# Two decoder layers on one core: a written opening, the block diagonal of the keys by ScalarE, and the first inverses' lower blocks between pieces of the second group's values

## The chip, the cores and the metric

The kernel runs on one core of a Trainium2 chip. The metric is the device time of one execution in microseconds; the time of a kernel is the median of several runs. A core has TensorE (PE, matmuls; PEld is its weight load), VectorE (DVE), ScalarE (ACT), GpSimd (POOL) and SyncE (SP), which issues all DMAs of this kernel. Each engine works through its own queue in order.

## The reference

A trunk of two layers works on x, 256 tokens by 2048 columns, in float32. Cut to what matters:

```python
h = _rmsnorm(x, gains[0])
# layer 0: combined projection 2048 -> 4096: q | k | v (8 differential heads) and u (S5 input)
proj = h @ w_in
m = concatenate([_diff_attention(q, k, v, ...), _s5(u, ...)]) @ w_out
# layer 1: RWKV-7 time mixing, 32 heads of 64
w_log = -softplus(-(w0 + tanh(xw @ w1) @ w2)) - 0.5
decay = exp(-exp(w_log))
a = sigmoid(a0 + (xa @ a1) @ a2)
kk = heads(k * k_k); kk = kk / max(norm(kk), 1e-12)
k = k * (1 + (a - 1) * k_a)
state = state * w_t + sa * b_t + v_t * k_t        # sa = state @ (-kk_t), b_t = kk_t * a_t
# every layer
x = x + _rmsnorm(m, gains[1])
x = x + _rmsnorm(_swiglu(_rmsnorm(x, gains[2]), ...), gains[3])
```

## The kernel before

**Weights.** All weight matrices are packed on the host into chunks of eight 128x128 blocks in the order of use. `chunk_load` (L358) loads one chunk of 512 KB into `wr` (SP), rounds it to a high half `wh` on ScalarE (L367), and takes the low half `wl = wr - wh` on VectorE (L368), or on POOL for the gate weights. Each of the three tags has three buffers. Activations are split into halves by `split` (L440): ScalarE writes the high one (L446), VectorE the low one (L450 or L452). Every product is then three matmuls: high x high, high x low, low x high.

**Order.** The instructions are written in program order with priorities (`high_priority`), and a list scheduler puts them into the queues of the engines; it also hands out the buffers of each tag. `strict = True` keeps TensorE's instructions in the order in which they are written. `fill(n)` in the values stage issues pieces of other work until n units are spent; a piece (one block row for one half of the tokens, three matmuls of 512 columns) is worth 2. Priorities of `mid()` and `hi()` put work ahead of what is written before it.

**The opening** (`even`, L818). x comes transposed, in five loads with the first three chunks between them (`LX`). For each of 16 row blocks, `split` makes the two halves with the gain, and `Acc.add` (L531) squares the block on ScalarE (L534) and adds the squares on POOL (L536). `rms_bc` (L459) sums them with eight matmuls, takes the power on POOL and spreads the result R over the partitions. `k_outer` (L432) multiplies the first four column blocks of u, 16 steps of 12 matmuls, into four PSUM banks. TensorE's order is not strict here. `s5_setup` (L948) computes the S5 coefficients from the constants `ce` by a chain of small VectorE operations, and `s5_tables` (L980) builds tables on POOL. Behind the opening, `main()` runs v, q, k and u tiles on TensorE while two side programs, attention and S5, are woken by counts of TensorE work (`SEQ`, `L0`, `LI`, `LS`).

**RWKV keys** (`rwkv_keys`, L1395). For each of 16 pairs of heads, `gates` (L1549) computes decays and factors into the tile `E` (tag H), and `pair` (L1592) multiplies the key projection into it. `pair` then builds a block diagonal `bd` of E (L1629, POOL; one buffer, since `NB = 1`), which TensorE multiplies with E to give the matrix `ak`, stored to DRAM (L1635). After pair 8 (`I0`), `inverse` (L1637) of the first half of the heads inverts the two diagonal 32x32 blocks of each ak by a chain of VectorE operations (L1661, L1662) in two buffers of the tag XI. `inverse2` (L1672) makes the lower block from them: twelve loads (L1681 to L1683) into two buffers of XI, 64 small matmuls, a copy, 64 more, a copy (L1699), and four stores (L1702). `I1 = 16` puts it behind the 16 pairs. Then come the values of the first group and `inverse` of the second half of the heads.

**RWKV values** (`rwkv_values`, L1729; TensorE strict). `chunk_in` (L1828) loads the inputs of one chunk of 64 tokens (T, CH, QB, MV), multiplies QB with CH and masks the result on VectorE; `chunk` (L1876) does the state's step. `FILL` lists the work that is put between: the other groups' values and the output projection. `chunk_in` of the first chunk is followed by `fill(FI)`, with `FI = 20`, then by the 16 chunk steps; the lower blocks of the second half come in step 6 (`S2`).

## Time and profile before

| what | value |
|---|---|
| median of 3 runs | 2608.89 us (2600.57 to 2609.81) |
| the profiled execution, its own time | 2606.43 us |
| its span, first to last instruction | 2604.6 us |
| mean granted TensorE clock | 0.975 |

All durations below come from the profiled execution. The page gives busy time by engine, a strip of 40 slices, the DMA queues, the chain of work that ended last, and the costliest groups of instructions by line. The other views used are the table of stretches (busy time of each engine between two moments, with the granted clock and what the DMA moved), the timeline (instructions in order of time; in brackets, how long the engine stood idle before it and what released it), the groups of one stretch by line, and the list of waits. "pg<-Z,wh" names the tile that an instruction writes and those that it reads; SPq is SyncE's queue of DMA issues. Matmuls overlap, so the distance of two starts says more than the duration of one. The engines idle most at these moments: the first 43 us, 76 to 320 us, and 1440 to 1565 us.

### The profile page before, as it was taken

The numbers are of one execution on the slowest core, as the hardware profiler recorded it, in microseconds if no ns is written. First come the engines' busy times: TensorE is split into PE (matmuls) and PEld (weight loads), VectorE is DVE, ScalarE is ACT, GpSimd is POOL, SyncE is SP. The second block draws the span as 40 slices with busy tenths as digits, with TensorE's granted clock in tenths as the row PEclk, the third lists the DMA queues.
The fourth block names the chain that finished last, engine by engine and source line by source line (L and its number), as shares of the span: only waits on it lengthen the run. The fifth ranks groups of instructions, "written<-read, shape, count | busy, mean of one in ns | idle before, by whom it ended". The sixth has DMA issues, their size and how long they took to land. (4 is left out here: it accounts for less than half of the span.)

```text
span 2604.6 us, 37350 instructions
## 1 busy us (share of the span) xinstructions
PE 2476.1 (95%) x14155; PEld 2081.8 (80%) x14155; DVE 1632.4 (63%) x2369; ACT 1205.3 (46%) x1808; POOL 408.3 (16%) x664
## 2 busy tenths in 40 slices
PE   7898799999999999998899889999999999999998
PEld 7786688788888888887799778887788888888886
DVE  7888985555555554445569978777555555555444
ACT  5343264644444444444666543443554444444433
POOL 4776621000000000000215630111100000000000
PEclk9898899999999999999999989999999999999999
DMA  6333256655555556664468677765555555555564
GB/s 218 114 114 103 80 178 199 203 187 186 192 187 186 192 186 200 200 224 161 154 216 248 206 224 197 207 200 171 202 187 186 189 190 186 186 190 190 194 206 162
DMA packets 221892, 481.93 MB, mean 185 GB/s; under 512 B 78736, under 2 KB 110736, under 8 KB 219920
## 3 DMA queue, kind: packets, MB, share of 16 engines
q1 hardware_dynamic: 221712, 479.55, 57.5%
q8 instruction: 111, 1.82, 0.3%
q14 instruction: 69, 0.57, 0.1%
HBM read 451.69 MB, written 27.79 MB: 184 GB/s over the span
## 5 line engine op out<-in xcount | busy, mean ns | idle before, releaser
L368 DVE TENSOR_TENSOR wl<-wr,wh 128x1024 fp32r<-128x1024 f32 x760 | 939.8, 1238 | 790.9 <-ACT wh L367 787.6
L367 ACT CAST wh<-wr 128x1024 fp32r<-128x1024 f32 x768 | 806.3, 1051 | 1023.7 <-PE pb L305 729.3
L305 PE MATMUL pg<-wh,Z 128*128 128x512 f32 x1664 | 641.2, 397 | 2.8 <-DVE Z L450 2.4
L305 PE MATMUL pb<-wh,Z 128*128 128x512 f32 x1408 | 554.0, 394 | 4.1 <-DVE Z L450 4.1
L305 PEld LDWEIGHTS pg<-wh,Z 128*128 128x128 f32 x1664 | 313.8, 189 | 72.8 <-issue 3.4
L305 PE MATMUL pg<-wl,Z 128*128 128x512 f32 x832 | 324.9, 391 | 0.4 <-DVE wl L368 0.4
L305 PEld LDWEIGHTS pb<-wh,Z 128*128 128x128 f32 x1408 | 264.9, 188 | 62.4 <-DVE Z L450 5.0
L305 PE MATMUL pb<-wl,Z 128*128 128x512 f32 x704 | 273.7, 389 | 0.0
L305 PE MATMUL pg<-wh,PP 128*128 128x512 f32 x576 | 225.6, 393 | 0.0
L305 PE MATMUL pb<-wh,PP 128*128 128x512 f32 x576 | 225.4, 393 | 0.0
L305 PEld LDWEIGHTS pg<-wl,Z 128*128 128x128 f32 x832 | 157.1, 189 | 34.5 <-DVE wl L368 1.2
L305 PE MATMUL pg<-wh,MX 128*128 128x512 f32 x504 | 174.9, 410 | 2.6 <-DVE X L1816 1.9
L305 PE MATMUL pg<-MX,wh 128*128 128x256 f32 x896 | 168.5, 286 | 6.7 <-ACT wh L367 4.0
L305 PE MATMUL pg<-Z,wh 128*128 128x256 f32 x736 | 146.3, 301 | 15.1 <-ACT wh L367 11.9
L305 PEld LDWEIGHTS pb<-wl,Z 128*128 128x128 f32 x704 | 132.5, 188 | 29.6
L305 PEld LDWEIGHTS pg<-MX,wh 128*128 128x128 f32 x896 | 139.9, 192 | 8.4 <-ACT wh L367 4.7
L305 PEld LDWEIGHTS pg<-Z,wh 128*128 128x128 f32 x736 | 120.5, 204 | 27.1 <-issue 14.8
L305 PE MATMUL pg<-MX,wl 128*128 128x256 f32 x448 | 128.1, 288 | 5.0 <-DVE wl L368 4.9
L305 PEld LDWEIGHTS pb<-wh,PP 128*128 128x128 f32 x576 | 108.2, 188 | 23.4
L305 PEld LDWEIGHTS pg<-wh,PP 128*128 128x128 f32 x576 | 108.2, 188 | 23.4
L500 POOL TENSOR_TENSOR ts<-ts,mhalf 128x1 f32<-128x1 f32 x6 | 3.3, 553 | 759.0 <-DVE ts L499 759.0
L305 PEld LDWEIGHTS pg<-wh,MX 128*128 128x128 f32 x504 | 96.7, 192 | 24.6 <-DVE X L1816 2.8
(429 smaller groups left out, 3639.1 us busy)
## 6 DMA issues: line engine op xcount, KB each, us to landing
wr<-wst SPq DMA_DIRECT2D x776, 512.0 KB, 3.4
dr<-H SPq DMA_DIRECT2D x16, 512.0 KB, 4.2
CH<-dr SPq DMA_DIRECT2D x16, 512.0 KB, 5.2
dr<-X SPq DMA_DIRECT2D x6, 1024.0 KB, 4.8
X<-dr SPq DMA_DIRECT2D x6, 1024.0 KB, 5.6
dr<-ak SPq DMA_DIRECT2D x16, 256.0 KB, 4.1
ln<-lnb SPq DMA_DIRECT2D x8, 512.0 KB, 4.7
S<-s5bc SPq DMA_DIRECT2D x4, 512.0 KB, 6.7
```

The lines of the kernel that those rows point to most:

```text
L305: self.pe(self.nc.tensor.matmul(out, lhsT, rhs, start=start, stop=stop))
L367: self.gated(nc.scalar.copy(h, r))
L368: self.gated((nc.gpsimd if pool else nc.vector).tensor_tensor(l, r, h.bitcast(F32), op=ALU.subtract))
L500: self.nc.gpsimd.tensor_tensor(r, ms, self.mhalf[:, 0:1], op=ALU.pow)
```

## The change

Four things are changed.

1. **The opening is written out.** TensorE's order is strict from the start. 54 (`W0`) matmuls on a tile of zeros come first. The split of row block k + 4 is written behind step k. The sum of squares is taken from x in row form: two loads of 1 MB (`cx`), two squares of 128x2048 on ScalarE with their sum, and the mean and power as columns; the 16 squares, 14 additions and 8 sum matmuls go. `behind` holds a DMA or an activation until a given chunk's load or cast has been issued on the same engine: the row loads behind chunks 3 and 4, `ce` behind 5, the first two S5 tables behind 6 and 7, the squares behind the casts of 4 and 5. `LX` now puts chunks 1 and 2 one place earlier among the blocks of x.
2. **The block diagonal** is copied by ScalarE (`BE = "a"`).
3. **The gates.** The scaling of the decay's exponent (L1568) leaves VectorE: ScalarE adds 1 and the factor goes into the scale of the three exponentials. L1577 goes: 1 is added inside L1578, and the factor -0.5 goes into a new column `nhk = -0.5 k_k`.
4. **The lower blocks of the first half** (`inverse2` of 0) move from the end of the keys to the start of the values, where their three parts alternate with fills of 10, 5 and 5; the first `chunk_in` now follows them and the 16 steps follow it directly. `inverse` of the second half is thereby written ahead of `inverse2` of the first.

```diff
-I1 = 16
-LX = ((0, 2), (0, 0), (2, 2), (4, 4), (1, 0), (8, 4), (2, 0), (12, 4))
+LX = ((0, 2), (0, 0), (2, 2), (1, 0), (4, 4), (2, 0), (8, 4), (12, 4))
+W0 = 54
-BE = "g"
+BE = "a"
...
+    def behind(self, ins, c):
+
+        for a in self.chunks[c]:
+            if a.ins.engine == ins.ins.engine:
+                self.after(ins.ins, a.ins)
...
-            ce = self.load_const("ce", self.slot("ce", 1, shape=[P, self.lay["ce"][1]]))
-            acc = Prog.Acc(self)
+            self.strict = STRICT
+            u = self.arr("U", 1, 8)
+            cold = u[7][:, :P].bitcast(BF16)
+            gp.memset(cold, 0.0)
+            self.warm(W0, cold)
+            r2, ss = self.slot("r2", 1, shape=[P, 2]), self.slot("ssx", 1, shape=[P, 2])
+            xr = [self.mslots() for _ in range(2)]
+            rows = self.halves(xr)
+            steps = self.k_steps([("in", 24 + a) for a in range(4)], zH, zL)
+
+            def part(k):
+                self.split(zH[k], zL[k], x[k], self.gain(0, 0, k))
+
+            for k in range(4):
+                part(k)
             for k in range(KD):
-                self.split(zH[k], zL[k], x[k], self.gain(0, 0, k))
-                acc.add(x[k], k == KD - 1)
-            r2 = self.slot("r2", 1, shape=[P, 2])
-            _, R, R8 = self.rms_bc(acc.cur, half=0.125, col=r2)
-            u = self.arr("U", 1, 8)
-            us = self.k_outer([("in", 24 + a) for a in range(4)], zH, zL)
+                us = next(steps)
+                if k + 4 < KD:
+                    part(k + 4)
+                if k in (6, 8):
+                    t = k // 2 - 3
+                    self.behind(nc.sync.dma_start(rows[t], self.d["cx"][:, t * DM:(t + 1) * DM]), 3 + t)
+                if k == 10:
+                    ce = self.load_const("ce", self.slot("ce", 1, shape=[P, self.lay["ce"][1]]), 5)
+            for t in range(2):
+                self.behind(nc.scalar.activation(rows[t], rows[t], AF.Square, accum_out=ss[:, t:t + 1]), 4 + t)
+            ms = self.tmp("ts", [P, 2])
+            v.tensor_scalar(ms, ss, 1.0 / DM, 1e-6, op0=ALU.mult, op1=ALU.add)
+            gp.tensor_tensor(r2, ms, self.mhalf, op=ALU.pow)
+            self.strict = False
+            pr = self.spread(r2)
+            R, R8 = self.tmp("n"), self.tmp("n")
+            nc.scalar.activation(R, pr, AF.Copy)
+            nc.scalar.activation(R8, pr, AF.Copy, scale=0.125)
...
-        nc.sync.dma_start(flat[:, 1024:], self.d["s5bc"][qt])
+        i = nc.sync.dma_start(flat[:, 1024:], self.d["s5bc"][qt])
+        if qt < 2:
+            self.behind(i, 6 + qt)
...
+        co["nhk"] = cf[:, o + 704:o + 720]
+        v.tensor_scalar(co["nhk"], co["k_k"], -0.5, None, op0=ALU.mult)
...
-            if j == I1:
-                with self.mid():
-                    list(self.inverse2(co, po, 0, iv))
-        if I1 > 15:
-            with self.mid():
-                list(self.inverse2(co, po, 0, iv))
...
-            co["iv"] = self.inverse(co, po, 1)
+            co["iv"] = [iv, self.inverse(co, po, 1)]
...
-        v.tensor_scalar(ld, ld, e, e, op0=ALU.mult, op1=ALU.add)
+        nc.scalar.activation(ld, ld, AF.Identity, bias=1.0)
         v.tensor_tensor_scan(ld, co["reset"], ld, 0.0, op0=ALU.mult, op1=ALU.add)
-        nc.scalar.activation(Pv, ld, AF.Exp)
-        nc.scalar.activation(iv, ld, AF.Exp, scale=-1.0)
+        nc.scalar.activation(Pv, ld, AF.Exp, scale=e)
+        nc.scalar.activation(iv, ld, AF.Exp, scale=-e)
         gp.memset(E[:, :, 0, 0, 0:1], 1.0)
-        nc.scalar.activation(E[:, :, 0, 0, 1:], ch(ld)[:, :, :C - 1], AF.Exp)
+        nc.scalar.activation(E[:, :, 0, 0, 1:], ch(ld)[:, :, :C - 1], AF.Exp, scale=e)
...
-        v.tensor_scalar(ta, ta, -0.5, -0.5, op0=ALU.mult, op1=ALU.add)
-        v.tensor_tensor(E[:, :, 1, 0], ch(ta), ch(iv), op=ALU.mult)
+        v.scalar_tensor_tensor(E[:, :, 1, 0], ch(ta), 1.0, ch(iv), op0=ALU.add, op1=ALU.mult)
...
-            v.scalar_tensor_tensor(o, ch(k), col("k_k"), o, op0=ALU.mult, op1=ALU.mult)
+            v.scalar_tensor_tensor(o, ch(k), col("nhk" if i else "k_k"), o, op0=ALU.mult, op1=ALU.mult)
...
+        i2 = self.inverse2(co, po, 0, co["iv"][0])
+        with self.mid():
+            next(i2)
+        fill(FI // 2)
+        with self.mid():
+            next(i2)
+        fill(FI // 4)
+        with self.mid():
+            list(i2)
+        fill(FI // 4)
         with self.mid():
             cur = self.chunk_in(co, 0, 0, V)
...
-        fill(FI)
         for s in range(NG * NC_):
...
-            i2 = self.inverse2(co, po, 1, co["iv"]) if s == S2 else None
+            i2 = self.inverse2(co, po, 1, co["iv"][1]) if s == S2 else None
```

More of the change, by code (lines that the diff above doesn't have):

```diff
@@ L218, in __init__ @@
         self.strict, self.xw = False, []
-        self.ahead = {}
+        self.ahead, self.chunks = {}, {}
         self.alias = {}
@@ L249, in dbg, with load_const @@
             self.dbg_fn(self, name, ap)
-    def load_const(self, key, t):
+    def load_const(self, key, t, c=None):
         lay, width = self.lay[key]
-        self.nc.sync.dma_start(t, self.d[key])
+        i = self.nc.sync.dma_start(t, self.d[key])
+        if c is not None:
+            self.behind(i, c)
         return {n: t[:, o:o + w] for n, (o, w) in lay.items()}
@@ L305, in mm, with warm @@
         self.pe(self.nc.tensor.matmul(out, lhsT, rhs, start=start, stop=stop))
-    def warm(self, n):
+    def warm(self, n, w=None):
         if n:
-            w, ps = self.ident.bitcast(BF16), self.pa()
+            w, ps = self.ident.bitcast(BF16) if w is None else w, self.pa()
             for _ in range(n):
@@ L361, in chunk_load @@
             r = self.wp.tile([P, CB * P], F32, tag="wr", name=f"wr{c}")
-            nc.sync.dma_start(r, self.d["wst"][c])
+            ins = [nc.sync.dma_start(r, self.d["wst"][c])]
+            self.chunks[c] = ins
             if raw:
@@ L366, in chunk_load @@
             l = self.wp.tile([P, CB * P], F32R, tag="wl", name=f"wl{c}")
-            self.gated(nc.scalar.copy(h, r))
+            ins.append(nc.scalar.copy(h, r))
+            self.gated(ins[1])
             self.gated((nc.gpsimd if pool else nc.vector).tensor_tensor(l, r, h.bitcast(F32), op=ALU.subtract))
```

## The prediction

> **What bounds the kernel now.** I read the page's busy line first, then the table of stretches, then the timeline of the stretches where TensorE is not full.
>
> ```profile
> PE 2476.1 (95%) x14155; PEld 2081.8 (80%) x14155; DVE 1632.4 (63%) x2369; ACT 1205.3 (46%) x1808; POOL 408.3 (16%) x664
> ```
>
> TensorE is busy for 95% of the span, so nothing off TensorE is worth anything unless it fills one of its gaps. The table of stretches shows where the gaps that this change can touch lie (columns: start:end, then length, then busy time of PE, PEld, DVE, ACT and POOL, granted clock, DMA share, GB/s).
>
> ```profile
> 9.00:43.00 34.00, 29.46 (x202) 28.64 (x202) 31.90 (x80) 20.06 (x42) 11.29 (x14) 0.85 0.66 230
> 60.00:340.00 280.00, 236.38 (x1763) 199.95 (x1762) 244.23 (x520) 96.93 (x197) 187.49 (x329) 0.90 0.32 106
> 1420.00:1548.00 128.00, 114.20 (x844) 104.86 (x842) 118.51 (x238) 71.29 (x152) 66.53 (x80) 0.96 0.72 213
> 1546.50:1565.50 19.00, 9.42 (x283) 8.15 (x282) 3.29 (x6) 5.57 (x12) 2.20 (x5) 0.64 0.94 222
> ```
>
> The opening has 4.5 us of idle TensorE and a clock of 0.85; the S5 and attention stage behind it has 43.6 us of idle, with VectorE the busier engine (244 of 280 us); the end of the RWKV keys has 13.8 us, again with VectorE at 118.5 of 128; and the hand-over to the values has 9.6 us of idle at a clock of 0.64. These four places are what the change works on.
>
> **The opening.** The rows are TensorE's timeline, one row of VectorE's, the duration of the splits by line, two stretches, and the group of the earlier warm-up matmuls.
>
> ```profile
> 9.07 1.65 PE L305 MATMUL pg<-Z,wh 128*128 128x256 f32 x6 [9.07 <-ACT wh L367]
> 12.43 0.40 PE L305 MATMUL pg<-Z,wh 128*128 128x256 f32 x2
> 20.20 1.01 PE L305 MATMUL pg<-Z,wl 128*128 128x256 f32 x3 [1.66 <-DVE wl L368]
> 21.22 0.63 PE L305 MATMUL pg<-Z,wh 128*128 128x256 f32 x2
> 21.65 0.41 PE L305 MATMUL pg<-Z,wl 128*128 128x256 f32 x1
> 35.73 0.39 PE L305 MATMUL pa<-Z,wh 128*128 128x256 f32 x2
> 37.09 0.39 PE L305 MATMUL pa<-Z,wh 128*128 128x256 f32 x2
> 43.12 0.47 PE L305 MATMUL pg<-wh,Z 128*128 128x512 f32 x1
> ...
> 10.19 8.82 DVE L452 SCALAR_TENSOR_TENSOR Z<-X,cg,Z 128x256 fp32r<-128x256 f32 x10
> ...
> L452 DVE SCALAR_TENSOR_TENSOR Z<-X,cg,Z x16: 469/946/962, 5.3 to 23.8; 128x256 fp32r<-128x256 f32 x16
> ...
> 8.00:12.00 4.00, 2.93 (x13) 2.93 (x14) 2.95 (x4) 4.00 (x10) 1.96 (x3) 1.00 1.02 407
> 24.00:28.00 4.00, 4.00 (x28) 3.89 (x27) 3.90 (x11) 0.85 (x1) 0.00 (x0) 0.74 0.38 117
> ...
> 1203.22 6.18 PE L312 MATMUL pa<-cg 128*128 128x256 bf16 x55
> ```
>
> The 16 steps of u (12 matmuls each) run from 9.07 to about 43.0. At full clock a step takes 37.09 - 35.73 = 1.36 us, so 16 of them are 21.8 us; the other 12 us are two stalls and a slow clock. Two matmuls are 0.43 us apart (21.22 to 21.65), or 0.215 each, against 0.113 later: the pair that takes 0.40 at 12.43 takes 0.63 at 21.22. The clock rises 3.3 us after the first matmul, is lost again in the stall, and comes back about 26 us (a mean of 0.74 from 24 to 28 is half of that at half speed), 5.8 us after the unbroken run from 20.20 begins. VectorE runs ten splits in a block of 8.82 us ahead of the second wl, each 0.95 where the shortest takes 0.47, while POOL adds squares beside them.
>
> The new opening issues 54 matmuls on zeros before any weight is there. They need only a memset, so they start near 1 us. With 3.3 to 5.8 us at 0.215 (15 to 27 of them) and the rest at 6.18/55 = 0.112, they end between 8.7 and 9.8: about when the first cast is done (9.07), and the clock is then up. They cost nothing except in the later case, some 0.7 us. Program order on TensorE now puts the first wl matmul third instead of ninth: one wait of about a microsecond. Then the steps run at 1.36. Removed: 16 squares on ScalarE, 14 adds on POOL, 8 sum matmuls. Added: two squares over whole rows, the row form of x (2 MB) and, later in SP's queue than before, the constants ce and two S5 tables, each held behind a chunk. Chunk loads stand behind those holds, but each hold waits only for a load that stands ahead of it in the same queue. What it costs is bandwidth: to the last chunk about 9.8 MB must land (x 2, eight chunks 4, rows 2, tables 1, ce and gains 0.5), at 407 GB/s 24 us, from about 4 us on. An estimate by order of issue has chunks 4 and 5 land about 20 and 24 us, with cast and subtraction done 2 us behind that, so the steps wait some 2 us in all. The end: 9.1 + 1 + 21.8 + 2 = 34 us instead of 43.1, so **9 us earlier**. The squares end some 27 us and R is there before 34; if the row loads come 5 us later than I think, the evacuations wait and up to 5 of the 9 are lost.
>
> **How much of it is kept.** The stage behind it is not TensorE's alone.
>
> ```profile
> 24.15 0.17 DVE L724 TENSOR_SCALAR sm<-sm 128x32 f32<-128x32 f32 x1
> 57.65 0.19 DVE L977 TENSOR_TENSOR k<-sm,sm 128x32 f32<-128x32 f32 x1
> ...
> 70.19 0.78 POOL L1031 TENSOR_TENSOR S<-s,s 128x256 f32<-128x256 f32 x1
> ...
> PE pb L305 <- DVE s L1095: 14.0, 6, 8.8
> PE pa L305 <- DVE q L711: 11.0, 2, 6.3
> PE pg L305 <- DVE s L1059: 9.7, 4, 5.5
> ```
>
> The S5 setup is a chain of small VectorE operations; it got going at 24.15, ended at 57.65, and POOL's first table followed at 71. In the new kernel ce lands about 24 us, so the setup starts no earlier, and shares VectorE with the subtractions as before; one or two fewer fall into it. I expect the first table within 2 us of where it is. So S5 gains nothing, while TensorE arrives 9 us sooner at a stage in which it already waits 35 us for VectorE (the three rows). What can be kept is the work that does not need S5: the first attention head and the q, k tiles, which fill the gap that VectorE has before the table (its 36 us of idle in 60 to 340 is the reserve). Bounds: nothing kept or even 2 us lost if ce is later, all 9 kept. I take **4**, a little under the middle, since VectorE is the busier engine there.
>
> **Block diagonal and gates.** Groups by line, one stretch, then waits (in order: waiter, what it waited for, total us, times, longest).
>
> ```profile
> L1608 DVE SCALAR_TENSOR_TENSOR H<-KR,M,H 128x256 f32<-128x256 f32 x32 | 24.3, 791 | 0.1
> L1577 DVE TENSOR_SCALAR m<-m 128x256 f32<-128x256 f32 x16 | 8.3, 516 | 3.1 <-ACT m L1576 3.1
> L1568 DVE TENSOR_SCALAR m<-m 128x256 f32<-128x256 f32 x16 | 5.1, 317 | 0.0
> L1629 POOL COPY bd<-H 64x256 f32<-64x256 f32 x32 | 23.3, 727 | 25.9 <-PE pa L305 13.2 <-DVE H L1608 6.3 <-ACT m L1571 5.5
> L1847 ACT COPY VB<-X 64x256 f32<-64x256 f32 x32 | 12.9, 403 | 13.3 <-PE pb L305 12.9
> ...
> 1355.00:1548.00 193.00, 179.16 (x1395) 167.67 (x1393) 176.09 (x330) 114.18 (x244) 100.62 (x119) 0.97 0.74 224
> ...
> PE pa L305 <- POOL bd L1629: 4.7, 1, 4.7
> ACT m L1570 <- DVE M L1620: 12.6, 4, 5.0
> ```
>
> VectorE loses the 16 operations of L1577 and of L1568, 8.3 + 5.1 = 13.4 us; L1578 becomes a fused form, which I estimate at up to 0.1 more each, so 12 us net; by time (128 of 193 us) 8 of them fall after 1420. POOL loses 23.3 us, and with it the one wait of 4.7 us that TensorE has for bd. ScalarE gains 32 copies of the size of L1847 (12.9 us) and 16 activations, which I put at the same 0.40 each (6.4): 19 us over the 193 from 1355 to 1548, of which it is busy 114, so there is room in sum. The new column of k_k is one small operation. What is not free is ScalarE's order: a copy of bd waits for L1608 on VectorE, and the casts of later weight chunks stand behind it. TensorE's 13.8 us of idle bound the gain above; of them 4.7 go with POOL's copy, VectorE's 8 us should free 2 to 3 of the other 9, and the new waits on ScalarE give 2 back: **5**, with bounds of -5 (below) and 11. One rule bears on this. L1608 has a mean of 0.79 us. The Trainium skill (GPSIMD Engine Reference, section 1, Specifications) says that POOL shares its SBUF interfaces with VectorE and contends with VectorE instructions of two SBUF inputs. By it, and by the 0.47 that such an operation takes at the shortest, the copies' going would give VectorE up to 32 x 0.32 = 10 us more and the sum would be 3 to 5 us lower; but POOL keeps three more operations per pair, so I leave it out.
>
> **The lower blocks of the first inverses.** TensorE's timeline, then SP's.
>
> ```profile
> 1546.75 1.05 PE L305 MATMUL pa<-bd,H 128*128 128x128 f32 x8
> 1550.88 1.35 PE L305 MATMUL pb<-XI 32*32 32x32 f32 x122 [0.79 <-DMA XI<-dr]
> 1562.77 2.05 PE L305 MATMUL pa<-QB,CH 128*128 128x128 f32 x8 [2.48 <-DMA QB<-dr]
> 1573.93 1.05 PE L305 MATMUL pb<-VB,MV 128*128 128x128 f32 x8
> ...
> 1541.03 2.25 SPq L1681 DMA_DIRECT2D XI<-dr x4
> 1550.58 0.90 SPq L1635 DMA_DIRECT2D dr<-ak x2
> ```
>
> Today the last pair's matmuls end at 1547.8. Then come the two halves of the lower blocks and what they wait for, the first chunk's inputs (QB), 10 pieces (a fill of 20) of the second group's values, and the first chunk at 1573.93. In the change five pieces stand ahead of the first half, three ahead of the second and the rest behind it. A piece is three matmuls of 512 columns, twice 0.113 each: 0.68 us. From 1547.8: 10 pieces 6.8, two halves 1.4 each, so TensorE gets to the first chunk's inputs at 1557.5. Those inputs (QB) land at 1562.8 today; their loads stand in SP's queue where they stood, so it waits 5 us there. Then 2.0 for QB and the transposes behind it, and 2 more for three mask operations on VectorE (an estimate from L1608's 0.79), which the pieces used to hide and nothing hides now: 1566.8. That is **7 us** sooner than 1573.93. The load of T stands behind four stores and two landings: about 1568 by estimate, needed at 1569. If QB lands sooner, up to 5 more; if T lands 4 us later, 4 less.
>
> **The sum.** 4 + 5 + 7 = 16 us. The profiled execution took 2606.4 (span 2604.6), so 2590.4, which is 0.7% under the median shown, 2608.9. The runs of before differ by 9 us, and 0.5% (13 us) is about what a measurement can tell from no change.
>
> **Rivals.**
> *VectorE swallows the opening.* If S5's first table sets the whole stage, nothing of the 9 arrives: 2606.4 - 12 = 2594. For it: the 35 us of waits; against it: the 36 us in which VectorE itself has nothing to do there. Chance 0.2.
>
> *ScalarE's queue becomes the bound of the keys.* POOL's copies sat idle 6.3 us for L1608 and 13.2 for the single bd buffer. On ScalarE such a wait holds the casts; three chunk buffers, of two steps or 2.7 us each, cover some. If half of these 20 us reach TensorE, the keys lose 5 instead of winning 5: 2600. ScalarE already sits in such waits (12.6 us in four) and TensorE survives most. Beside it stands the Trainium skill (TensorE: Matmul & The Clock Gate, Architectural detail): ScalarE and VectorE are strict first-in, first-out. By that rule, nothing can pass a waiting copy, and those 12.6 us agree. Chance 0.17.
>
> *The second inverses take the two XI buffers first (the slower end).* inverse(1) is now written ahead of inverse2(0), and both use the tag XI with two buffers.
>
> ```profile
> L1661 DVE TENSOR_TENSOR XI<-XI 128x30 f32<-128x30 f32 (+14 forms) x30 | 12.9, 429 | 0.7
> L1662 DVE TENSOR_TENSOR XI<-XI,XI 128x30 f32<-128x30 f32 (+14 forms) x30 | 9.9, 328 | 0.6
> ```
>
> If buffers go by the order of writing, the first half waits until inverse(1) is through: start about 1564 (its loads stand behind the ak stores of 1550.58, and what is loaded there lands by 1562.77), 26 us of VectorE (22.8 in the two rows, and an estimated 3 for both ends), then loads that today take from 1541.03 to 1550.88: 1600 in place of 1551. Nothing but five pieces is there to fill it. Behind it stand two halves, five pieces, QB and masks, 10 us, so the first chunk starts at 1610, 36 late: 2606.4 + 36 - 9 = 2633. It decides as soon as the last pair's ak is stored before the first inverses are done. Against it: today the loads of A are issued at 1541.03, the last two stores of ak at 1550.58, 9 us later, and loads do pass earlier-written ones that are not ready. Chance 0.1.
>
> *The zeros do not raise the clock.* Then 54 x 0.215 = 11.6 us delay the first step to 12.6 and the first steps run slow: 5 of the 9 are gone, 2 fewer kept: 2592. Chance 0.05.
>
> **The numbers.** Forecast 2590, chance 0.48, its own range 2579 to 2600. The low end of the whole is all terms at their best (9 + 11 + 8: 2578, and 2 for the measurement), the high end ScalarE's rival with nothing kept of the opening and 2 lost, 2607, and 5 for the median's spread; the XI rival stays outside: 2576 to 2612. Faster by over 0.5% (under 2596): most of the forecast, half of the first rival and the last, 0.55; within, 0.32; slower, 0.13: the XI rival and a little of an unforeseen order, since a change of priorities moves instructions elsewhere.
>
> **What would show it.** Right: the first 512-column matmul near 34 us and matmuls 0.113 apart from the first step; the first S5 table still about 70; the whole stage ending some 4 us sooner; no wait of TensorE for bd; ScalarE's waits for L1608 short; first-half matmuls among pieces of values about 1551 less the gain so far. Wrong: u still ending after 38, the table later than 75, ScalarE idle in front of bd for over 2 us at a time with TensorE stalled behind, or 30 us of idle before the first chunk.

## The result and the profile after

The changed kernel takes 2628.15 us (median of 4 runs, 2624.74 to 2631.24), the kernel before in the same session 2607.3 (2600.57 to 2609.81). The ratio is 1.0081, with a 95% interval of 1.0069 to 1.0093: slower by 0.8%, about 21 us. The forecast was 2590 with a range to 2612, so the time lies outside. One rival had foreseen it, that of the XI buffers: 2633, with a chance of 0.1 and left outside the range.

The busy line of the changed kernel's page:

```profile
PE 2474.4 (94%) x14201; PEld 2078.6 (79%) x14201; DVE 1625.3 (62%) x2338; ACT 1221.2 (47%) x1844; POOL 367.4 (14%) x619
```

Its table of stretches at the four places of the prediction (columns as there):

```profile
9.00:43.00 34.00, 31.18 (x227) 28.67 (x228) 27.62 (x73) 22.74 (x34) 0.72 (x1) 1.00 0.86 328
60.00:340.00 280.00, 233.45 (x1719) 197.81 (x1719) 243.23 (x519) 92.41 (x191) 186.67 (x336) 0.88 0.30 99
1420.00:1540.00 120.00, 109.16 (x825) 99.93 (x824) 113.42 (x219) 81.39 (x184) 48.79 (x58) 0.99 0.76 227
1540.00:1590.00 50.00, 8.72 (x151) 6.95 (x150) 27.40 (x68) 5.83 (x10) 3.47 (x6) 0.58 0.55 132
```

The opening is fuller and from its first step at full clock (matmuls 0.113 apart), the keys end sooner, and then comes a hole: of the 50 us behind 1540, TensorE works 8.7. TensorE's timeline shows one wait in it:

```profile
1537.91 1.05 PE L307 MATMUL pa<-bd,H 128*128 128x128 f32 x8
...
1543.85 0.40 PE L307 MATMUL pg<-wh,MX 128*128 128x512 f32 x1
1581.81 0.28 PE L307 MATMUL pb<-XI 32*32 32x32 f32 x2 [37.57 <-DMA XI<-dr]
...
1597.72 1.13 PE L307 MATMUL pb<-VB,MV 128*128 128x128 f32 x8 [1.31 <-DVE MV L1898]
```

The last pair's matmuls end 8.8 us earlier than before (they start at 1537.91 in place of 1546.75). The five pieces in front of the first half end at 1544.24, and the first half then waits 37.57 us for its loads. The first chunk comes at 1597.72, which is 23.8 us later than before. What held the loads stands in the timeline of SP (SPq is a DMA's issue):

```profile
1529.29 1.40 SPq L1701 DMA_DIRECT2D dr<-XI  x1
1540.13 0.33 SPq L1667 DMA_DIRECT2D dr<-ak  x1
1544.89 1.86 SPq L1683 DMA_DIRECT2D XI<-dr  x2
...
1574.00 1.66 SPq L1697 DMA_DIRECT2D dr<-XI  x2
1575.90 1.66 SPq L1701 DMA_DIRECT2D dr<-XI  x1
1578.87 0.34 SPq L1713 DMA_DIRECT2D XI<-dr  x1
```

and in that of VectorE, the first and the last step of the second half's inverse:

```profile
1549.74 1.23 DVE L1687 TENSOR_TENSOR XI<-XI,dl 128x1024 f32<-128x1024 f32 x1 [2.92 <-DMA XI<-dr]
...
1574.01 1.86 DVE L1698 TENSOR_TENSOR XI<-XI,dl 64x1024 f32<-64x1024 f32 x1
```

The inverse of the first half was finished and its store issued at 1529.29. From about then its lower blocks could have been loaded (in e2 below they are, from 1534). Their loads (L1713) go out at 1578.87, directly behind the stores of the *second* half's inverse (1574.00, 1575.90), whose own loads waited until 1544.89, 4.4 us of it for the last ak store (issued at 1540.13) to land. Between lies VectorE's chain, 1549.74 to 1575.87. It is the sequence that the rival described.

Where the 19.6 us of longer span (2624.2 against 2604.6) come and go: the warm matmuls behind the even stage start at 452.90 instead of 453.85, those behind the SwiGLU of layer 0 at 1202.28 instead of 1203.22, the keys end 8.8 us sooner, the first chunk starts 23.8 later, and the warm matmuls behind the values come at 1856.02 instead of 1836.49, 19.5 later. The rest of the program is as long as it was.

### The profile page after: what moved, and what is told of

The parts are those of the page before. It is cut to its first block, busy times and chain, and to the rows that moved or that the text cites. A ratio compares the mean times of both kernels' runs of the same rounds, so it can differ in the third digit from the quotient of the medians.

```text
span 2624.2 us, 37358 instructions
## 1 busy us (share of the span) xinstructions
PE 2474.4 (94%) x14201; PEld 2078.6 (79%) x14201; DVE 1625.3 (62%) x2338; ACT 1221.2 (47%) x1844; POOL 367.4 (14%) x619
## 4 chain that ended last, share of the span: by engine, by line
PE 78%; DVE 9%; issue 5%; ACT 3%; POOL 3%; DMA 1%; SPq 0%; DVEq 0%; ACTq 0%; POOLq 0%
PE pg L307 44%; PE pb L307 31%; DVE wl L378 2%; PE pa L307 2%; PE pa L709 1%; DVE s L1096 1%; ACT wh L376 1%; DMA wr<-wst 1%; DVE X L1118 0%; DVE s L1132 0%; DVE M L1118 0%; ACT MX L1442 0%; DVE sm L1114 0%; DVE MX L460 0%; POOL s L1043 0%
## 5 line engine op out<-in xcount | busy, mean ns | idle before, releaser
L307 PEld LDWEIGHTS pg<-Z,wh 128*128 128x128 f32 x736 | 121.2, 204 | 20.1 <-issue 19.5
L307 PE MATMUL pg<-wl,PP 128*128 128x512 f32 x288 | 111.8, 388 | 0.0
```

The source lines that it names most:

```text
L307: self.pe(self.nc.tensor.matmul(out, lhsT, rhs, start=start, stop=stop))
```

## The experiments

All times of place are read from the timelines of TensorE. The warm matmuls are groups like the one that the prediction shows at 1203.22; they stand in front of a new stage, the first behind the even stage (the opening with attention and S5). "Keys" is the time from the warm matmuls in front of layer 1 to the end of the last bd matmul, "values" the time from there to the warm matmuls behind the values. "Chunk 1, 2, 8" are the starts of these chunks' first matmuls (pb<-VB,MV). Ratios are to the kernel before in the same session, where it took 2606.3 to 2608.8 us.

| kernel | median | ratio, 95% interval | keys | chunk 1 | chunk 2 | chunk 8 | values |
|---|---|---|---|---|---|---|---|
| before | 2607.3 | 1 | 344.6 | 1573.9 | 1588.2 | 1677.8 | 288.7 |
| the change | 2628.15 | 1.0081 (1.0069 to 1.0093) | 336.7 | 1597.7 | 1612.4 | 1697.4 | 317.1 |
| e1 second pass back | 2608.75 | 1.0001 (0.9990 to 1.0011) | 336.9 | 1569.5 | 1584.3 | 1676.9 | 298.1 |
| e2 own buffers | 2604.56 | 0.9985 (0.9976 to 0.9994) | 336.8 | 1560.2 | 1584.0 | 1675.0 | 296.8 |
| e3 order | 2604.77 | 0.9984 (0.9972 to 0.9995) | 340.0 | 1561.8 | 1582.4 | 1677.3 | 294.0 |
| e4 opening alone | 2609.41 | 1.0006 (0.9995 to 1.0016) | 345.9 | 1570.8 | 1588.8 | 1678.7 | 290.2 |
| e5 opening and gates | 2608.65 | 1.0007 (0.9996 to 1.0018) | 344.5 | 1571.2 | 1585.1 | 1679.5 | 292.5 |
| e7 order, cold | 2598.32 | 0.9970 (0.9959 to 0.9981) | 339.4 | 1560.9 | 1581.8 | 1672.2 | 290.2 |
| e8 store by ACT | 2606.67 | 0.9999 (0.9990 to 1.0007) | 336.8 | 1557.3 | 1575.1 | 1675.0 | 296.5 |
| e9 constants first | 2603.54 | 0.9986 (0.9975 to 0.9996) | 338.7 | 1561.6 | 1581.1 | 1676.3 | 293.7 |
| e10 own buffers, ACT | 2598.53 | 0.9961 (0.9946 to 0.9975) | 342.5 | 1565.3 | 1585.1 | 1676.0 | 288.6 |
| e11 the same, cold | 2596.20 | 0.9952 (0.9940 to 0.9965) | 336.7 | 1561.7 | 1581.5 | 1668.9 | 287.4 |
| e12 opening alone, cold | 2605.01 | 0.9992 (0.9980 to 1.0003) | 343.8 | 1573.3 | 1588.6 | 1678.4 | 290.4 |
| e13 e10, old opening | 2601.43 | 0.9970 (0.9961 to 0.9980) | 337.0 | 1563.7 | 1584.7 | 1671.0 | 289.9 |

The places come from one profiled execution of each kernel, so a difference of a few us between two rows is no evidence by itself: e2 and e10, whose keys are written alike, differ by 5.7 us there.

### Is it the buffers?

**e1** (the second pass is `inverse2`): the lower blocks go back to the end of the keys; opening, block diagonal and gates stay.

```diff
+        with self.mid():
+            list(self.inverse2(co, po, 0, iv))
         for _ in self.values(vv, 0, Vs[:, 0]):
...
-        i2 = self.inverse2(co, po, 0, co["iv"][0])
...
+        fill(FI)
         for s in range(NG * NC_):
```

> The changed kernel with one part undone: the lower blocks of the first half (inverse2(0)) are written again behind the last pair of the keys stage, ahead of the first values and of inverse(1), and the 20 filler pieces again stand in one row behind the first chunk's loads. Theory (the two XI buffers are handed out in the order of writing, so inverse2(0), written behind inverse(1), waits for it): the wait of TensorE on XI of 37.6 us is gone, the first chunk's py starts some 24 us earlier relative to the end of the keys than in the changed kernel, no later than 26.2 us behind the last bd matmul as in the kernel before; the time is 2607 - 7 = 2600 us (2597 to 2603), the 7 being what opening and keys brought until 1545 us in the changed kernel's profile. Rival (the filler pieces between the halves, not the buffers, cost the time): also faster than the changed kernel, but then the run with buffers of its own stays slow. Rival (the cost is in the opening or the keys, as a delay that shows later): the time stays near 2628.

The wait is gone and the first chunk comes 28.2 us earlier than in the change. The time is 2608.75, though, not 2600: what the keys won, the values stage lost (298.1 us in place of 288.7). That is taken up below.

**e2**: the order of writing stays as in the change; only the two tiles of the first half's lower blocks come from another tag.

```diff
-        A, W = (self.slot("XI", 2, shape=[P, 2, 16, B], pool=po) for _ in range(2))
+        if hf:
+            A, W = (self.slot("XI", 2, shape=[P, 2, 16, B], pool=po) for _ in range(2))
+        else:
+            AW = self.slot("MX", 8, shape=[P, 2, 2, 16, B], pool=po)
+            A, W = AW[:, 0], AW[:, 1]
```

> The changed kernel, its order of writing kept; only A and W of inverse2(0) are taken from one MX buffer, which is free once the keys are done, in place of two XI buffers. Theory (the XI buffers): the loads of inverse2(0) go out directly behind the last ak store (1540 us) in place of 1578.9, the wait of 37.6 us goes, the first half starts behind the five pieces at about 1545 and the first chunk's py at about 1567; the time is about 2594 us (2588 to 2600). Rival (the order of the queue or of VectorE: inverse(1), written first, goes first in any case): loads and wait stay where they are, 2628. The two are 34 us apart.

The first loads in SP's timeline of this run, then TensorE's, the first and second half and the product with T:

```profile
1534.03 0.86 SPq L1719 DMA_DIRECT2D MX<-dr  x2
...
1543.75 1.29 PE L307 MATMUL pb<-MX 32*32 32x32 f32 x128
1549.57 1.42 PE L307 MATMUL pb<-MX 32*32 32x32 f32 x128 [2.27 <-ACT MX L1727]
...
1570.82 1.94 PE L307 MATMUL pb<-gs,T 64*64 64x64 f32 x16 [5.37 <-DMA T<-dr]
```

The first half runs without any wait behind its five pieces, 38 us earlier than in the change, and 128 matmuls in one row, since all loads are there. With nothing else altered, this settles the cause: the loads were held by the buffers, not by the data, SP's queue or VectorE. The loads go out from 1534 on, ahead of the last ak stores, which the argument against the rival had as a general habit of loads. They do so once they have a buffer. The time is 2604.56: the rival of the expectation is out by 24 us, and the expected 2594 is missed by 10. The first chunk is 13.7 us ahead of before, the second 4.2: between them lie the 5.37 us for T and a slow clock behind that wait (the last section has the rows).

**e3**: the two XI buffers stay; `inverse` of the second half is written behind the second half of the lower blocks.

```diff
-        with self.mid():
-            co["iv"] = [iv, self.inverse(co, po, 1)]
+        co["iv"] = [iv]
...
             list(i2)
+            co["iv"].append(self.inverse(co, po, 1))
```

> The changed kernel with inverse(1) written behind the second half of inverse2(0) in place of ahead of it; the XI buffers stay two. Theory (buffers go in the order of writing): the wait of 37.6 us goes as with buffers of its own, inverse(1) itself starts some 20 to 25 us later and is not needed before the seventh chunk; 2594 us (2588 to 2601). Rival (VectorE's chain of inverse(1), 25 us long, now falls on the first chunks and delays them): 2605 to 2615, with waits of TensorE on the first chunk's VectorE results of over 10 us in sum. Rival (the order of writing does not matter): 2628.

The first loads in SP's timeline, and TensorE's first half:

```profile
1535.55 0.87 SPq L1712 DMA_DIRECT2D XI<-dr  x2
...
1544.80 1.29 PE L307 MATMUL pb<-XI 32*32 32x32 f32 x128
```

The same time as with buffers of its own, 2604.77. Order alone decides who gets the buffers. Here too the expected 2594 is missed. In this run the lead is 9.4 us at the seventh chunk's start and 0.6 at the eighth's, so what was left of it goes where the second half's blocks are needed.

### Where the rest of the gain went

In e1 the keys end 10.7 us earlier than in the kernel before, but the first chunk starts only 4.4 earlier. The timeline of SP in e1:

```profile
1546.93 0.62 SPq L1879 DMA_DIRECT2D QB<-dr  x1
1553.36 1.82 SPq L1685 DMA_DIRECT2D XI<-dr  x2
1555.23 1.61 SPq L1880 DMA_DIRECT2D MV<-dr  x1
1556.88 0.62 SPq L1879 DMA_DIRECT2D QB<-dr  x1
```

TensorE's in the same place:

```profile
1552.91 0.34 PE L307 MATMUL pb<-XI 32*32 32x32 f32 x9 [0.93 <-issue]
1559.44 2.05 PE L307 MATMUL pa<-QB,CH 128*128 128x128 f32 x8 [6.19 <-issue]
```

The loads of the second half's inverse (L1685) need an XI buffer and are issued at 1553.36, as soon as the matmuls of the second half of the lower blocks are done with it (1553.25). For 5.8 us nothing else leaves SP's queue, and behind them stands the other load of QB (1556.88), for which the first chunk's matmuls are the next to wait: 6.19 us ("issue" is a wait whose releaser the profile doesn't show; that it is QB is read from the order of the two timelines). So the same two buffers seem to cost in the old order of writing too; there they hold a queue, and in the new one the blocks themselves. This is read and not tested, and it is not so in the kernel before, whose two loads of QB left at 1553.02 and 1554.70, ahead of the inverse's loads at 1560.39.

**e8**: e3, with the four stores of the lower blocks issued by ScalarE and not by SP.

```diff
-            nc.sync.dma_start(Tf[0:B, i, B:2 * B], A[r, 0])
+            (nc.sync if hf else nc.scalar).dma_start(Tf[0:B, i, B:2 * B], A[r, 0])
```

> The run with inverse(1) behind the second halves; the four stores of the lower blocks of half 0 are issued by ScalarE, directly behind its copy, and no more by SP behind the first chunk's loads. There the copy ended at 1556.2 and the stores were issued at 1560.2 to 1563.0, and TensorE waited 4.6 us for T. Theory (what is left of the lead at the hand-over is lost to SP's order): the wait for T falls by 3 to 4 us, the clock that the idle time lowers falls less, and the second chunk's py starts 4 us earlier or more; 2601 us (2597 to 2604) if that lead is kept, 2605 if the seventh chunk takes it back as it took 9 us in the run before. Rival (the transfers of small packets themselves fill the DMA engines at 0.85 of their time, so the T loads land no earlier): the wait for T stays over 3 us, 2605.

The wait for T falls from 4.57 to 3.15 us and the second chunk starts 7.3 us earlier than in e3. None of it lasts: the eighth chunk is at 1675.0, and the time is that of before, 2606.67. Two rows show where it went. VectorE's last step of the second half's inverse:

```profile
1644.29 2.02 DVE L1697 TENSOR_TENSOR XI<-XI,dl 64x1024 f32<-64x1024 f32 x1
```

TensorE's first lower blocks of that half, which are written into the seventh chunk:

```profile
1658.43 0.31 PE L307 MATMUL pb<-XI 32*32 32x32 f32 x2 [11.51 <-DMA XI<-dr]
```

Written late, the second inverse is done only at 1646.3; its store goes out at 1647.55, the loads of the lower blocks from 1649.88, and TensorE, now earlier, waits 11.51 us for them. It is the rival of e3's expectation, that VectorE's chain is late, but at the seventh chunk and not at the first, and with SP's queue as a part of it. In e2 the same chain ended at 1601.6.

**e10**: e2 (own buffers, so the second inverse may stay early) with ScalarE's stores.

> The run with buffers of its own, with the four stores of the lower blocks of half 0 issued by ScalarE behind its copy. In the run with buffers of its own the stores went out at 1559.7 behind the loads of the first chunk, TensorE waited 5.4 us for T, and the second chunk's py came at 1584.0; inverse(1) was done at 1601.6 there, so that, other than with inverse(1) written late, the seventh chunk has its lower blocks in time. Theory (the lead of the hand-over lasts where neither T nor the second half's blocks are late): the second py at 1575 to 1578, no wait of over 4 us for XI at the seventh chunk, and the warm matmuls behind the values at 1828 to 1831 in place of 1835.3; the time 2599 us (2596 to 2602). Rival (the values stage has a wait for each that is removed, whatever its place): second py as above, but the warm matmuls at 1834 or later and 2604.

The time is what was expected, 2598.53, a ratio of 0.9961 (0.9946 to 0.9975). The places were not: the second chunk came at 1585.1, the warm matmuls at 1833.1, and ScalarE issued late (ACTq is an issue by ScalarE; the copy that the stores carry away ended at 1556.5):

```profile
1560.87 3.27 ACTq L1738 DMA_DIRECT2D dr<-MX  x3
1564.37 0.59 ACT L1911 COPY tk<-pa 128x512 f32<-128x512 f32 x1 [7.88 <-DMA dr<-MX]
```

TensorE's product with T in the same run:

```profile
1572.53 1.93 PE L307 MATMUL pb<-gs,T 64*64 64x64 f32 x16 [3.99 <-DMA T<-dr]
```

The wait for T is 4.0 us still. This profiled execution (2602.96) is the slowest of the kernel's six, and its keys ended 6 us later than e2's at a lower granted clock (0.93 from 1450 to 1500 and 0.91 from there to 1540, against 0.97 and 1.00), so it holds only part of the gain. Behind the keys the values take 288.6 us, against 296.8 in e2; e11 and e13, which have the same buffers and stores, take 287.4 and 289.9. So the gain lies in the values stage, but only 1.4 us of it is the wait for T. What the other 7 are is not taken apart: e2 has, besides, a wait of 4.12 us for a copy of ScalarE at 1627 and a pair of chunks 19.4 us apart, and e10 has 1.3 and 15.9 there.

### The parts of the change by themselves

**e4**: the kernel before with the new opening alone. **e5**: the same with the new gates, block diagonal still by GpSimd.

> The kernel before with the new opening alone: block diagonal by GpSimd, the old gates, and the old place of inverse2(0). Theory: the first matmul of 512 columns starts some 7.5 us earlier (35.7 in place of 43.1), the first S5 table does not, and at the warm matmuls behind the even stage (452 us) some 1 us is left; 2606 us (2603 to 2608), the same as before within what can be measured. Rival (my prediction's 4 us kept): 2603. Rival (the opening costs the time of the whole change): 2628.

> The run with the second pass back, with the block diagonal made by GpSimd again: the new opening and the new gates, nothing else of the change. It tells which part moved the end of the keys. There the last bd matmul ends 686.3 us behind the warm matmuls of the even stage with the full keys part (450.88 to 1537.15) and 695.3 without it (452.94 to 1548.24), so 9.0 to be shared. Theory (my prediction's terms: the gates bring what the 4.7 us of the wait for bd do not): the wait of TensorE for bd stays, and some 5 of the 9 us go, the keys end 691 behind the warm matmuls. Rival (bd on ScalarE brings nearly all): 694 to 695. Rival (the gates bring nearly all): 687. The time itself is 2607 to 2610 in all three, as an earlier end of the keys has brought nothing in the run with the second pass back.

The opening alone, with its zeros, changes nothing that can be measured (1.0006). The gates by themselves don't shorten the keys: 344.5 us, as before (344.6). With ScalarE's bd as well they take 336.7 to 342.5 in ten profiles (the change, e1 to e3, e7 to e11 and e13), against 343.8 to 345.9 in the four without (before, e4, e5, e12). So it is ScalarE's block diagonal, with the new gates in place, that brings the 7.6 us of e1 against e5 (6.6 between the means of the ten and the four). No run has ScalarE's copies with the old gates. Two views of e5 say why the gates alone don't shorten the keys. From the list of waits of TensorE in the keys (total us, times, longest):

```profile
PE pg L307 <- DVE wl L378: 12.7, 8, 3.4
```

From the groups by line of VectorE in the same stretch:

```profile
L1642 DVE SCALAR_TENSOR_TENSOR H<-KR,M,H 128x256 f32<-128x256 f32 x32 | 27.9, 904 | 0.8 <-ACT KR L1637 0.6
```

In before the wait for wl was 5.2 us (seven times) and that for bd 4.7; in e5 the wait for bd is gone, and that for wl is 12.7. VectorE lost 13.4 us of operations, but the same 32 operations on H now take 27.9 us where they took 24.3, the fused form of L1578 takes 12.0 where that took 9.1, and its busy time from 1355 to the end of the keys falls by 1.7 only (175.9 to 174.2). So e5's theory is out and its first rival holds: the keys end 693.9 us behind the warm matmuls (1547.25 less 453.35), and its numbers were 694 to 695.

**e9**: e3, with the constants ce loaded ahead of the rows cx.

```diff
-                if k in (6, 8):
-                    t = k // 2 - 3
-                    self.behind(nc.sync.dma_start(rows[t], self.d["cx"][:, t * DM:(t + 1) * DM]), 3 + t)
-                if k == 10:
-                    ce = self.load_const("ce", self.slot("ce", 1, shape=[P, self.lay["ce"][1]]), 5)
+                if k == 6:
+                    ce = self.load_const("ce", self.slot("ce", 1, shape=[P, self.lay["ce"][1]]), 3)
+                if k in (8, 10):
+                    t = k // 2 - 4
+                    self.behind(nc.sync.dma_start(rows[t], self.d["cx"][:, t * DM:(t + 1) * DM]), 4 + t)
...
-                self.behind(nc.scalar.activation(rows[t], rows[t], AF.Square, accum_out=ss[:, t:t + 1]), 4 + t)
+                self.behind(nc.scalar.activation(rows[t], rows[t], AF.Square, accum_out=ss[:, t:t + 1]), 5 + t)
```

> The run with inverse(1) behind the second halves; in the opening the constants ce are loaded ahead of the rows cx (behind chunk 3, not 5). Theory (the opening's lead of 7.5 us is lost because ce lands at 25.0 in place of 20.1 us, so that the chain of small VectorE operations, and with it GpSimd's first S5 table, end 3.2 us later than in the kernel before): ce lands at about 21, the first table ends at 70 to 71 in place of 74.2, and the warm matmuls behind the even stage start 2 to 4 us earlier, at 447 to 449; the time 2602 us (2598 to 2605). Rival (another thing holds the stage, GpSimd's whole chain up to 125 us or the attention): the first table is earlier and 451 stays; 2605. Rival (the squares, now later, delay R): the first 512-column matmul 2 us later or more, 2607.

GpSimd's end of the first S5 table, from the timeline of the change:

```profile
73.42 0.77 POOL L1068 TENSOR_TENSOR S<-s,s 128x256 f32<-128x256 f32 x1
```

The same from the timeline of e9:

```profile
63.07 0.71 POOL L1068 TENSOR_TENSOR S<-s,s 128x256 f32<-128x256 f32 x1
```

And e9's row in the table of stretches:

```profile
60.00:340.00 280.00, 231.72 (x1721) 195.43 (x1721) 248.13 (x522) 93.16 (x194) 177.40 (x310) 0.88 0.30 101
```

The table is ready 10 us earlier and the even stage still ends at 453.2, against 453.85 in the kernel before and 450.9 in e3. The first table therefore doesn't set this stage. What does is not shown by a run; VectorE is the fullest engine there with 248 of 280 us.

**e7, e11, e12**: e3, e10 and e4 without the 54 matmuls on zeros.

```diff
-W0 = 54
+W0 = 0
```

> The run with inverse(1) behind the second halves, without the 54 zero matmuls (W0 = 0). Theory: the first steps of the opening wait for weights and inputs, not for the clock; the first matmul of 512 columns starts at 36 to 38 us, and as the stage behind it is held by the S5 tables, the warm matmuls at its end start at 451 to 453 as with the zeros; the same time, 2605 us (2602 to 2608). Rival (the zeros carry the opening): the first 512-column matmul at 40 or later, and 2607 to 2609.

> The run before in this list without the 54 zero matmuls (W0 = 0). With inverse(1) written late, taking them away gave a ratio to the kernel before of 0.9970 (0.9959 to 0.9981) in place of 0.9984 (0.9972 to 0.9995), a difference that the intervals do not tell apart. Theory (the zeros bring nothing and cost nothing): the same as the run before in this list within 0.1 %. Rival (the zeros cost 2 to 4 us, by a clock that is granted lower behind them): 0.1 to 0.15 % faster than it.

> The run with the opening alone, without the zeros (W0 = 0). That had a ratio of 1.0006 (0.9995 to 1.0016). Theory (the opening is worth nothing behind the even stage, with or without zeros): 0.9995 to 1.0010. Rival (the zeros cost 2 to 4 us): 0.9990 to 0.9995.

In the change the zeros do what they were meant to do, and the first 512-column matmul follows at 35.66:

```profile
1.11 7.86 PE L314 MATMUL pa<-U 128*128 128x256 bf16 x54 [1.11 <-POOL U L844]
10.35 0.39 PE L307 MATMUL pg<-Z,wl 128*128 128x256 f32 x1 [0.76 <-DVE wl L378]
...
35.66 0.39 PE L307 MATMUL pg<-wh,Z 128*128 128x512 f32 x1
```

In e7, without them, the first two steps run at half the pace (0.215 between two starts, up to 15.36), and the 512-column matmuls begin as early:

```profile
9.24 0.79 PE L307 MATMUL pg<-Z,wh 128*128 128x256 f32 x2 [9.24 <-ACT wh L376]
...
15.15 0.41 PE L307 MATMUL pa<-Z,wl 128*128 128x256 f32 x1
15.36 0.48 PE L307 MATMUL pg<-Z,wh 128*128 128x256 f32 x2
...
35.37 0.40 PE L307 MATMUL pg<-wh,Z 128*128 128x512 f32 x1
```

What the warm start wins in the first 6 us it waits away for wl later (five waits, 2.7 us in sum, in the change). All three kernels without zeros are a little faster than their partners: by 0.14, 0.09 and 0.14%. Each of these differences is inside its own interval, and e7 and e12 ran in other sessions than their partners. That the zeros bring nothing is shown, that they cost some 3 us is likely, and by what way they would is open. e7's expectation (2605) was missed by 7, and no row of the opening accounts for it; its profiled execution, 2602.27, is the slowest of its seven and so holds little of the gain.

**e13**: e10 with the opening of the kernel before.

> The first run of this list with the opening of the kernel before: the keys and the hand-over of the change, with buffers of its own and ScalarE's stores. Theory (the opening's 7.5 us earlier first stage leave 1 to 3 us at 452 us and nothing that can be measured in the end): the same as the first run of this list within 0.15 %, 2597 to 2604. Rival (the opening is worth its 3 us): 2602 to 2605, some 0.12 % slower than the first run.

0.9970 against 0.9961 for e10: the two intervals overlap. But the old opening has no zeros either, and against e11, the new opening without zeros in the same session, the medians lie 5 us apart (2601.43 and 2596.20, the intervals 0.9961 to 0.9980 and 0.9940 to 0.9965). By itself the new opening without zeros gave 0.9992 (0.9980 to 1.0003) in e12. So with the zeros it is worth nothing to 3 us, and without them some 2 to 5, which these runs make likely and don't settle.

## Why the prediction was wrong

**The failed step is the argument against the third rival.** The prediction put the XI buffers at 0.1, since "loads do pass earlier-written ones that are not ready". The row it used, A's loads at 1541.03 ahead of the ak stores at 1550.58, shows that a load may stand in SP's queue ahead of stores written earlier. It says nothing about who gets a buffer. In the kernel before, the lower blocks of the first half were written ahead of the second inverse and so had the buffers by any rule; the row couldn't tell the two apart. The runs did: with a tag of their own (e2) or written first (e3) the blocks load without delay, and the change as written has the 37.57 us of idle TensorE that the prediction named as a sign of being wrong ("30 us of idle before the first chunk"). The rival's own sum came near, 2633 for 2628, with errors both ways. It had the first half at 1600, or 1591 with the 9 us of opening and keys that it takes off at the end; measured is 1581.81, since the chain starts at 1549.74 (1555 by the same count) and the loads behind it take 5.9 us and not 10. The chain itself takes 26.1, as forecast. From the first half to the first chunk it then takes 15.9 us in place of 10, and the stage wins back 4.3 of the 23.8 us by its end.

**The hand-over, 7 us sooner.** This term failed twice. In the change the first chunk came 23.8 later. Where the buffers are free (e2, e3) the first chunk comes 12 to 14 us sooner than before, of which 9 and 7.5 are the keys' end; behind the end of the keys it is 21.7 and 21.5 us, against 26.1, so the move itself brings 4.5. The prediction's late T, "4 less", came: 4.57 and 5.37 us of waiting. What it didn't have was that the lead must last to the end of the values: in e2 9.5 of 13.7 us go between the first and the second chunk, in e3 and e8 most of it at the seventh, where the second half's blocks are needed at a time that VectorE and SP set. At the end of the stage at most 1.3 of the 7 us is left in any profile: the values take 288.7 us before and 287.4 to 289.9 in e10, e11 and e13, more in e2 and e3.

**The keys, 5.** 7.9 in the change (344.6 to 336.7), and these are two of its rows. From the groups by line in the keys:

```profile
L1640 DVE SCALAR_TENSOR_TENSOR H<-KR,M,H 128x256 f32<-128x256 f32 x32 | 27.1, 880 | 0.0
```

From the list of waits:

```profile
ACT bd L1659 <- DVE H L1640: 6.9, 7, 3.5
```

The wait for bd went, as it was costed. VectorE's 8 us were no gain at all by themselves. The 10 us more that VectorE was to get by the rule of the Trainium skill on the shared SBUF interfaces (GPSIMD Engine Reference, section 1, Specifications) did not come, and it was right to leave them out: with the new gates in both, an operation on H takes 0.904 us with GpSimd's copies (e5) and 0.879 with ScalarE's (e1), 0.8 us in sum. The rule itself agrees with the traces; it is other work of GpSimd that these operations meet. In the timeline of the change:

```profile
1365.03 2.51 POOL L378 TENSOR_TENSOR wl<-wr,wh 128x1024 fp32r<-128x1024 f32 x1 [3.95 <-ACT wh L376]
1367.50 0.92 POOL L1642 TENSOR_TENSOR rk<-rk,KR 128x256 f32<-128x256 f32 x1
...
1365.25 3.44 DVE L1640 SCALAR_TENSOR_TENSOR H<-KR,M,H 128x256 f32<-128x256 f32 x2
...
1491.42 0.87 DVE L1640 SCALAR_TENSOR_TENSOR H<-KR,M,H 128x256 f32<-128x256 f32 x2
```

Two operations take 3.44 us beside these two of GpSimd, and 0.87 at 1491.42, where GpSimd does nothing. In the opening, where GpSimd's additions went, VectorE's 16 splits take 0.479 us each in place of 0.803. The rival that ScalarE holds its queue for bd is refuted as a loss: ScalarE waits 6.9 us for H in seven pieces, 3.5 at most, and the keys still end earlier.

**The opening, 9 raw and 4 kept.** 7.5 raw (35.66 for 43.12), 0.95 kept; in the profiles with the new opening the even stage ends between 450.9 and 453.5, against 453.85 and 453.36 (e13) with the old one. The first rival was right in its result and wrong in its reason: it made the first S5 table the limit, and e9 has that table 10 us earlier for nothing. The table was also not "within 2 us of where it is" but 3.2 later: VectorE first used ce at 20.07 in the kernel before and had to wait for it until 25.01 in the change.

**The sum.** With the buffers free and nothing else altered (e2) the change brings 4 us (0.15%) instead of the 16 forecast; so the buffers are the step that made it slower, and the terms of the opening and the hand-over were too large besides. With ScalarE's stores (e10) it brings 10 us (0.39%), and 12.5 without the zeros (e11, 0.9952), most of it the keys' 7.9. That is the best version found: the block diagonal by ScalarE, the blocks between the pieces in buffers of their own, no zeros.

## What to carry to other kernels

Before a piece of work is moved ahead of or behind another, list the buffers that both use: if a tag is handed out in the order of writing, the move also changes who waits for whom, and a row that shows loads overtaking stores is no evidence on that. A lead won in one stage is kept only until the next place at which something else sets the time, so look for that place first (here the second half's blocks at the seventh chunk) and for the queue that stands still in front of it. A start made warm brought nothing here, where the data arrived no sooner.

## What was not expected of the hardware

The clock falls to half within a wait and stays low behind it. In e2, around the 5.37 us for T, the stretches of TensorE read (busy, granted clock, DMA share, GB/s):

```profile
1565.00:1570.00 5.00, 0.44 (x2) 0.80 0.87 227
1570.00:1575.00 5.00, 4.18 (x22) 0.50 0.86 312
1575.00:1580.00 5.00, 5.00 (x45) 0.68 0.20 45
```

Five us at 0.50 and five at 0.68 lose 4.1 us by estimate, so the wait of 5.37 costs about 9.5, which is what the lead over the kernel before falls by from the first chunk to the second (13.7 to 4.2). If the clock is at half until it rises, 0.68 puts the rise at 1578.2, 7.4 us behind the first matmul at 1570.82. Cold starts differ: read from the distance of the starts, the clock rises 3.4 us after the first matmul in the kernel before (9.07 to 12.43) and 6.1 us after it in e7 (9.24 to 15.36). The Trainium skill (TensorE: Matmul & The Clock Gate, Part 1) puts that time at about 3.4 us of sustained work and calls it variable from run to run; the kernel before agrees, and the other two places took about twice that. The granted clock of the table doesn't show the cold start: for e7 it reads 1.00 from 9 to 15.3 us, where the matmuls are 0.215 apart.

A DMA issued by ScalarE is not free for it. In e8 three issues stand in its queue from 1553.45 to 1557.38, and the next copy, whose data were ready at 1555.95, starts at 1557.47, 1.5 us late. In e10 the three take 3.27 us and start 4.4 us behind the copy that they carry away, for a reason that the trace doesn't show; the 7.88 us before the next copy are not their cost there, since its data were ready only at 1564.28.
